# A log-sum-exp kernel: loads of one size first, more single rows last, one activation table, and results stored in two column blocks

## The chip, the core and the metric

The kernel runs on one core of a Trainium2 chip. The time is device time of one execution in microseconds (us). The profile of an execution covers a span that is about 1.8 us shorter than that time: the profiled execution of the kernel before took 169.63 us and has a span of 167.86 us. Engines that matter here: ScalarE (ACT in the profile) computes the exponentials, VectorE (DVE) sums, SyncE (SP) issues the DMAs.

## The reference

The input is 32 x 512 rows of 1024 float32 values, 67.1 MB. For each row the result is the logarithm of the sum of exponentials.

```python
max_x = np.max(x, axis=-1, keepdims=True)
return (max_x.squeeze(-1) + np.log(np.sum(np.exp(x - max_x), axis=-1))).astype(np.float32)
```

Both kernels leave the maximum out. The values are normally distributed, so the exponentials don't overflow.

## The kernel before

Each of the 128 partitions holds 128 rows. The rows are loaded in chunks into a pool of ten buffers. A chunk of one row takes one Exp with an accumulated sum. Chunks of two or four rows are processed in pairs: one Exp runs over two rows and accumulates the sum of both, VectorE sums the first row alone, and one subtract at the end gives all the second sums. Then come two Lns and four stores.

```python
    head = [1, 1, 2, 2]
    tail = [2, 2, 2, 2, 1, 1]
    # ... sizes = head + [4] * 28 + tail; xs is a pool of 10 buffers
    for c0, rpc in sched:
        x_tile = xs.tile([P, RPC, D], fp32)
        nc.sync.dma_start(out=x_tile[:, 0:rpc, :], in_=x3[:, c0 : c0 + rpc, :])
        if rpc == 1:
            nc.scalar.activation(..., func=AF.Exp,
                accum_out=sums3[:, c0 // 2, (c0 % 2) : (c0 % 2) + 1])
            continue
        for k in range(rpc // 2):
            # ... Exp over rows lo, lo+1, accum_out=pair_buf[:, j : j + 1]
            # ... nc.vector.reduce_sum of row lo into sums3[:, j, 0:1]
    # ... one tensor_sub for all pairs; Ln over 126 columns, Ln over 2 columns
    for q in range(4):
        eng = nc.scalar if (q % 2 == 0) else nc.sync
        # ... eng.dma_start of 32 partitions x 128 columns (512 bytes a row)
```

The softmax here doesn't subtract the row's maximum and nothing guards it: scores larger than these inputs give would overflow.

## Time and profile before

| | before |
|---|---|
| median time | 169.27 us (169.19 to 169.29, 3 runs) |
| profiled execution: time, span | 169.63 us, 167.86 us |
| ScalarE, VectorE busy | 76%, 45% of the span |
| end of the input stream | 160.78 us |
| end of the last Exp with its accumulator read | 162.89 us |
| issue of the last result stores begins | 164.63 us |

The first fence has lines of the page of the kernel before: DMA busy tenths and GB/s in 40 slices of the span, the chain that ended last, and two groups of instructions (busy us, mean ns; then idle us of the engine before them and what ended it).

```profile
DMA  5999999999999999999999999999999999999910
GB/s 172 387 445 426 437 429 433 437 418 426 429 429 429 429 437 422 429 420 429 429 429 437 422 426 426 429 428 429 433 426 426 426 429 426 433 412 420 404 41 16
...
DMA x_tile<-in_x_dram 83%; ACT x_tile L72 8%; SPq L57 2%; DVE sums L78 2%; ACT x_tile L60 1%; ACT L95 1%; ACT result_buf L95 0%; ACT result_buf L101 0%; ACTq L72 0%
...
L72 ACT ACTIVATE x_tile<-x_tile 128x2048 f32<-128x2048 f32 x62 | 117.8, 1901 | 33.3 <-DMA x_tile<-in_x_dram 33.3
...
L95 ACT ACT_TABLE_LOAD x1 | 1.3, 1283 | 0.0
```

The DMA is full from the second slice to the 38th, at about 428 GB/s, and the chain is 83% input DMA. ScalarE spends 33.3 us waiting for input: it is faster than the stream. So the stream sets the length, and only what comes before it is at full rate and after its last byte can be shortened. A second table load (L95) of 1283 ns stands before the first Ln.

The next fence is the tail of the kernel before, from the timeline: start, duration, engine, line, operation; in brackets the idle time before it and what ended that.

```profile
158.81 1.91 ACT L72 ACTIVATE x_tile<-x_tile 128x2048 f32<-128x2048 f32 x1 [0.39 <-DMA x_tile<-in_x_dram]
...
160.72 1.04 ACT L60 ACTIVATE x_tile<-x_tile 128x1024 f32<-128x1024 f32 x1
...
161.76 1.04 ACT L60 ACTIVATE x_tile<-x_tile 128x1024 f32<-128x1024 f32 x1
...
162.70 0.19 ACT L60 ACTIVATION_READ_ACCUMULATOR x_tile<-x_tile 128x1 f32 x1
162.91 1.28 ACT L95 ACT_TABLE_LOAD   x1
164.20 0.31 ACT L95 ACTIVATE result_buf<-sums 128x126 f32<-128x126 f32 x1
164.42 0.19 ACT L101 ACTIVATE result_buf<-sums 128x2 f32<-128x2 f32 x1
164.63 0.82 SPq L111 DMA_DIRECT2D out_dram<-result_buf  x2
164.63 0.87 ACTq L111 DMA_DIRECT2D out_dram<-result_buf  x2
```

The last wait for data ends at 158.81 us. After that ScalarE has one pair and two single rows to do, loads a table, runs two Lns, and only then are the stores issued. Two windows of the stream (length, busy time by engine, clock, DMA share, GB/s):

```profile
20.00:50.00 30.00, 14.99 (x13) 23.53 (x26) 0.00 (x0) 1.00 1.01 430
50.00:100.00 50.00, 25.25 (x21) 39.40 (x41) 0.00 (x0) 1.00 1.01 428
```

### The profile page before, as it was taken

The page shows a single profiled execution, that of the slowest core. Times are in us where ns is not written, and L with a number is a line of the kernel's source. Part 1 is how long each engine was busy: PE and PEld are TensorE (multiplying, and loading weights), DVE is VectorE, ACT ScalarE, POOL GpSimd, SP SyncE. Part 2 cuts the span into 40 slices and gives each one's busy share as a digit, 9 for nine tenths or more (in the row PEclk, how much of TensorE's full clock was granted, in tenths as well). Part 3 has the DMA queues.
Part 4 walks back from the last instruction along what each step waited for, and adds up shares of the span by engine and source line. Part 5 has one row for each costly group of instructions (what it writes and reads, how often), then busy time and mean ns, then how long its engine had stood idle before and what let it go on. Part 6 is the DMA issues. An engine that isn't in the chain of part 4 may idle for free.

```text
span 167.9 us, 372 instructions
## 1 busy us (share of the span) xinstructions
DVE 75.8 (45%) x63; ACT 128.1 (76%) x136; POOL 0.2 (0%) x4
## 2 busy tenths in 40 slices
DVE  0022445445544544554454455444455544446630
ACT  3573897777789777778977777896777798779992
POOL 0000000000000000000000000000000000000000
DMA  5999999999999999999999999999999999999910
GB/s 172 387 445 426 437 429 433 437 418 426 429 429 429 429 437 422 429 420 429 429 429 437 422 426 426 429 428 429 433 426 426 426 429 426 433 412 420 404 41 16
DMA packets 5666, 67.19 MB, mean 400 GB/s; under 512 B 672, under 2 KB 800, under 8 KB 1312
## 3 DMA queue, kind: packets, MB, share of 16 engines
q1 hardware_dynamic: 5568, 67.14, 94.9%
q10 hardware_dynamic: 96, 0.03, 0.1%
q14 instruction: 2, 0.02, 0.0%
HBM read 67.11 MB, written 0.07 MB: 400 GB/s over the span
## 4 chain that ended last, share of the span: by engine, by line
DMA 83%; ACT 10%; SPq 2%; DVE 2%; issue 1%; ACTq 0%
DMA x_tile<-in_x_dram 83%; ACT x_tile L72 8%; SPq L57 2%; DVE sums L78 2%; ACT x_tile L60 1%; ACT L95 1%; ACT result_buf L95 0%; ACT result_buf L101 0%; ACTq L72 0%
## 5 line engine op out<-in xcount | busy, mean ns | idle before, releaser
L72 ACT ACTIVATE x_tile<-x_tile 128x2048 f32<-128x2048 f32 x62 | 117.8, 1901 | 33.3 <-DMA x_tile<-in_x_dram 33.3
L78 DVE TENSOR_REDUCE sums<-x_tile 128x1 f32<-128x1024 f32 x62 | 75.6, 1220 | 86.5 <-ACT x_tile L72 86.5
L72 ACT ACTIVATION_READ_ACCUMULATOR x_tile<-x_tile 128x1 f32 x62 | 11.6, 186 | 0.0
L60 ACT ACTIVATE x_tile<-x_tile 128x1024 f32<-128x1024 f32 x4 | 4.2, 1048 | 2.5 <-DMA x_tile<-in_x_dram 2.4
L60 ACT ACT_TABLE_LOAD x1 | 1.3, 1283 | 0.7 <-PEq L129 0.7
L95 ACT ACT_TABLE_LOAD x1 | 1.3, 1283 | 0.0
L60 ACT ACTIVATION_READ_ACCUMULATOR x_tile<-x_tile 128x1 f32 x4 | 0.7, 187 | 0.0
L95 ACT ACTIVATE result_buf<-sums 128x126 f32<-128x126 f32 x1 | 0.3, 308 | 0.0
L87 DVE TENSOR_TENSOR sums<-pair_buf,sums 128x62 f32<-128x62 f32 x1 | 0.2, 227 | 0.0
L101 ACT ACTIVATE result_buf<-sums 128x2 f32<-128x2 f32 x1 | 0.2, 187 | 0.0
L129 POOL MEMSET const-bfloat16-1.0<- 128x1 bf16 x1 | 0.1, 102 | 0.0
L129 POOL MEMSET const-uint8-127<- 128x1 uint8 x1 | 0.1, 102 | 0.0
L129 POOL MEMSET const-float32-1.0<- 128x1 f32 x1 | 0.1, 99 | 0.0
L129 POOL MEMSET const-float32-0.0<- 128x1 f32 x1 | 0.1, 98 | 0.2 <-issue 0.2
## 6 DMA issues: line engine op xcount, KB each, us to landing
x_tile<-in_x_dram SPq DMA_DIRECT2D x28, 2048.0 KB, 39.1
x_tile<-in_x_dram SPq DMA_DIRECT2D x6, 1024.0 KB, 30.7
x_tile<-in_x_dram SPq DMA_DIRECT2D x4, 512.0 KB, 13.3
out_dram<-result_buf SPq DMA_DIRECT2D x2, 16.0 KB, 1.5
out_dram<-result_buf ACTq DMA_DIRECT2D x2, 16.0 KB, 1.6
```

The costliest lines, as they stand in the source:

```text
L57: nc.sync.dma_start(out=x_tile[:, 0:rpc, :], in_=x3[:, c0 : c0 + rpc, :])
L60: nc.scalar.activation(out=x_tile[:, 0, :], in_=x_tile[:, 0, :], func=AF.Exp, accum_out=sums3[:, c0 // 2, (c0 % 2) : (c0 % 2) + 1],)
L72: nc.scalar.activation(out=x_tile[:, lo : lo + 2, :], in_=x_tile[:, lo : lo + 2, :], func=AF.Exp, accum_out=pair_buf[:, j : j + 1],)
L78: nc.vector.reduce_sum(out=sums3[:, j, 0:1], in_=x_tile[:, lo, :], axis=X,)
L87: nc.vector.tensor_sub(out=sums3[:, first_p : last_p + 1, 1], in0=pair_buf[:, first_p : last_p + 1], in1=sums3[:, first_p : last_p + 1, 0],)
L95: nc.scalar.activation(out=result_buf[:, 0:split_col], in_=sums_flat[:, 0:split_col], func=AF.Ln,)
L101: nc.scalar.activation(out=result_buf[:, split_col:rows_per_part], in_=sums_flat[:, split_col:rows_per_part], func=AF.Ln,)
L129: nc = _bacc.Bacc("TRN2", target_bir_lowering=False, num_devices=1)
```

## The change

The change intends to shorten both ends. It starts with 4-row loads, ends with four single rows instead of two, loads one table set that holds Exp and Ln before anything else, finishes the first 96 columns in the middle of the stream (own buffers, subtract, Ln), and leaves 32 columns for the end. The results go out in two stores on SyncE, the first of which is issued before the end.

```diff
-    head = [1, 1, 2, 2]
-    tail = [2, 2, 2, 2, 1, 1]
+    N_BULK = 29
+    N_TAPER = 4
+    N_SINGLE = 4
+    A_CHUNKS = 24
 ...
+    nc.scalar.preload_act_table_set("natural_log_exp_and_others")
+    # 24 chunks of 4 rows, into sumsA and pairA
+    nc.vector.tensor_sub(out=sumsA[:, :, 1], in0=pairA, in1=sumsA[:, :, 0])
+    nc.scalar.activation(out=resultA, in_=sumsA, func=AF.Ln)
+    # 5 chunks of 4 rows, 4 of 2 rows into sumsC and pairC, one tensor_sub,
+    # 4 single rows into sumsC
+    nc.scalar.activation(out=resultC, in_=sumsC, func=AF.Ln)
 ...
-    for q in range(4):
-        eng = nc.scalar if (q % 2 == 0) else nc.sync
-        p0 = q * PQ
-        eng.dma_start(out=out_view[p0 : p0 + PQ, :], in_=result_buf[p0 : p0 + PQ, :])
+    nc.sync.dma_start(out=out_view[:, 0:A_COLS], in_=resultA)
+    nc.sync.dma_start(out=out_view[:, A_COLS:rows_per_part], in_=resultC)
```

More of the change, by code (lines that the diff above doesn't have):

```diff
@@ L32, with load, do_pair_chunk @@
     RPC = 4
-    head = [1, 1, 2, 2]
-    tail = [2, 2, 2, 2, 1, 1]
-    n_bulk = (rows_per_part - sum(head) - sum(tail)) // RPC
-    assert sum(head) + n_bulk * RPC + sum(tail) == rows_per_part
-    sizes = head + [RPC] * n_bulk + tail
-    sched = []
-    c = 0
-    for s in sizes:
-        sched.append((c, s))
-        c += s
-        assert s == 1 or c % 2 == 0, "pair-style chunks must stay pair aligned"
-    singles = ctx.enter_context(tc.tile_pool(name="singles", bufs=1))
-    sums3 = singles.tile([P, n_pairs, 2], fp32)
-    pair_buf = singles.tile([P, n_pairs], fp32)
-    result_buf = singles.tile([P, rows_per_part], fp32)
-    pair_style = [False] * n_pairs
+    N_BULK = 29
+    N_TAPER = 4
+    N_SINGLE = 4
+    assert N_BULK * RPC + N_TAPER * 2 + N_SINGLE == rows_per_part
+    A_CHUNKS = 24
+    A_PAIRS = A_CHUNKS * RPC // 2
+    C_PAIRS = n_pairs - A_PAIRS
+    A_COLS = 2 * A_PAIRS
+    singles = ctx.enter_context(tc.tile_pool(name="singles", bufs=1))
+    sumsA = singles.tile([P, A_PAIRS, 2], fp32)
+    pairA = singles.tile([P, A_PAIRS], fp32)
+    resultA = singles.tile([P, 2 * A_PAIRS], fp32)
+    sumsC = singles.tile([P, C_PAIRS, 2], fp32)
+    pairC = singles.tile([P, C_PAIRS], fp32)
+    resultC = singles.tile([P, 2 * C_PAIRS], fp32)
     xs = ctx.enter_context(tc.tile_pool(name="xs", bufs=10))
-    for c0, rpc in sched:
+    def load(c0, rpc):
         x_tile = xs.tile([P, RPC, D], fp32)
         nc.sync.dma_start(out=x_tile[:, 0:rpc, :], in_=x3[:, c0 : c0 + rpc, :])
-        if rpc == 1:
-            nc.scalar.activation(
-                out=x_tile[:, 0, :],
-                in_=x_tile[:, 0, :],
-                func=AF.Exp,
-                accum_out=sums3[:, c0 // 2, (c0 % 2) : (c0 % 2) + 1],
-            )
-            continue
+        return x_tile
+    def do_pair_chunk(x_tile, c0, rpc):
         for k in range(rpc // 2):
             j = c0 // 2 + k
-            pair_style[j] = True
+            if j < A_PAIRS:
+                sums, pair, jj = sumsA, pairA, j
+            else:
+                sums, pair, jj = sumsC, pairC, j - A_PAIRS
             lo = 2 * k
@@ L75 @@
                 func=AF.Exp,
-                accum_out=pair_buf[:, j : j + 1],
+                accum_out=pair[:, jj : jj + 1],
             )
             nc.vector.reduce_sum(
-                out=sums3[:, j, 0:1],
+                out=sums[:, jj, 0:1],
                 in_=x_tile[:, lo, :],
@@ L82 @@
             )
-    first_p = pair_style.index(True)
-    last_p = len(pair_style) - 1 - pair_style[::-1].index(True)
-    assert all(pair_style[first_p : last_p + 1])
+    nc.scalar.preload_act_table_set("natural_log_exp_and_others")
+    for i in range(A_CHUNKS):
+        c0 = i * RPC
+        do_pair_chunk(load(c0, RPC), c0, RPC)
     nc.vector.tensor_sub(
-        out=sums3[:, first_p : last_p + 1, 1],
-        in0=pair_buf[:, first_p : last_p + 1],
-        in1=sums3[:, first_p : last_p + 1, 0],
-    )
-    split_col = 2 * (last_p + 1)
-    sums_flat = sums3.rearrange("p j s -> p (j s)")
-    nc.scalar.activation(
-        out=result_buf[:, 0:split_col],
-        in_=sums_flat[:, 0:split_col],
-        func=AF.Ln,
-    )
-    if split_col < rows_per_part:
+        out=sumsA[:, :, 1],
+        in0=pairA,
+        in1=sumsA[:, :, 0],
+    )
+    nc.scalar.activation(out=resultA, in_=sumsA, func=AF.Ln)
+    for i in range(A_CHUNKS, N_BULK):
+        c0 = i * RPC
+        do_pair_chunk(load(c0, RPC), c0, RPC)
+    for t in range(N_TAPER):
+        c0 = N_BULK * RPC + 2 * t
+        do_pair_chunk(load(c0, 2), c0, 2)
+    C_BULK_PAIRS = C_PAIRS - N_SINGLE // 2
+    nc.vector.tensor_sub(
+        out=sumsC[:, 0:C_BULK_PAIRS, 1],
+        in0=pairC[:, 0:C_BULK_PAIRS],
+        in1=sumsC[:, 0:C_BULK_PAIRS, 0],
+    )
+    for r in range(N_SINGLE):
+        c0 = N_BULK * RPC + 2 * N_TAPER + r
+        jj = c0 // 2 - A_PAIRS
+        x_tile = load(c0, 1)
         nc.scalar.activation(
-            out=result_buf[:, split_col:rows_per_part],
-            in_=sums_flat[:, split_col:rows_per_part],
-            func=AF.Ln,
-        )
-    PQ = P // 4
-    for q in range(4):
-        eng = nc.scalar if (q % 2 == 0) else nc.sync
-        p0 = q * PQ
-        eng.dma_start(
-            out=out_view[p0 : p0 + PQ, :],
-            in_=result_buf[p0 : p0 + PQ, :],
-        )
+            out=x_tile[:, 0, :],
+            in_=x_tile[:, 0, :],
+            func=AF.Exp,
+            accum_out=sumsC[:, jj, (c0 % 2) : (c0 % 2) + 1],
+        )
+    nc.scalar.activation(out=resultC, in_=sumsC, func=AF.Ln)
+    nc.sync.dma_start(out=out_view[:, 0:A_COLS], in_=resultA)
+    nc.sync.dma_start(out=out_view[:, A_COLS:rows_per_part], in_=resultC)
 _INS = ['x']
```

## The prediction

> **What bounds the kernel now.** The 67.1 MB input load. In the page's 40 slices the DMA row is full from the second slice to the thirty-eighth; the windows view shows 428 to 433 GB/s from 20 to 140 us. The waits view agrees: ScalarE waits 33.3 us for input, about 1 us per 2 MB tile, and the chain of waits is 83% input DMA. A row per partition arrives every 1.22 us (0.52 MB at 428 GB/s); ScalarE takes 0.95 us for it in a pair, 1.04 us alone. So only the head before full bandwidth and the tail after the last bytes can be shortened.
>
> Head (windows, 2 to 12 us): 391 GB/s on average, with loads of 1, 1, 2 and 2 rows first.
> Tail (timeline): the DMA thins out from 159.2 and stops near 160.8 us; the last pair of Exps starts at 158.81 (the last wait for DMA), two single Exps follow without a wait and end at 162.89; a table load takes 1.28 us, two Lns run 164.20 to 164.61, the stores are issued from 164.63 (two per queue, about 0.41 us each), and the span ends at 167.9.
>
> **What the change does.**
> - One table set with both Exp and Ln is loaded first; the table load before Ln goes: -1.28 us, all on the critical path. The Trainium skill (ScalarE: Activation LUTs, Table sets) says `natural_log_exp_and_others` holds both; its page gives a switch as about 1283 ns of load plus 1380 ns of drain. This trace has the 1.28 us but no such drain: the load starts 0.02 us after the last accumulator read.
> - Two final Lns become one over 32 columns: -0.2 us.
> - Four single rows last in place of two: the last pair lands about 2.5 us sooner. Estimate: pair at 156.3, then singles of 1.04 us, ending near 162.4: -0.45 us.
> - Head of 2 MB loads only: ScalarE starts near 7 us instead of 4.4, which is free, as it has slack. At 428 instead of 391 GB/s the first 10 us would give -0.4 us (uncertain; part of it is ramp).
> - Output: two stores on the SP queue. The first (96 columns) is issued behind the loads and is off the path. The second has one issue in place of two: -0.4 us. But its rows are 128 bytes, before 512: DMA: Bandwidth & Descriptors (Specifications) says that below 512 bytes the engine does read-modify-write; no run shows its cost yet; I allow +0.2 us.
> - The mid-stream subtract and Ln: ScalarE waits about 1.6 us (reduce 1.22, subtract 0.23, signals) and works 0.3 us. Loads keep eight DMAs in flight with ten buffers, so this doesn't stop the stream: 0.
>
> Sum: -1.28 - 0.2 - 0.45 - 0.4 - 0.4 + 0.2 = -2.5 us.
>
> **Predicted** 166.8 us, 80% range 165.8 to 168.0. Faster by over 2% (under about 165.95 us) 0.13; within 2% 0.86; slower 0.01.
>
> **What would show each step.** One table load in the groups, at the start. From the end of the last Exp to the issue of the last store 0.3 us instead of 1.74. From that issue to the end about 2.9 us instead of 3.3. DMA rate unchanged at 428 in the middle; the DMA stops near 160.4. ScalarE waits about 1.6 us once, near 125 us, and catches up within two tiles with no dip of GB/s. The last Exp ends near 162.
>
> **What would make it wrong.** Starting with 2 MB loads raises the rate more, or not at all; the small stores complete much later than I allow; the single rows arrive late at the tail (the engines finish unevenly), so each Exp waits; the mid-stream stall reaches the stream.

## The result

The changed kernel took 167.51 us (median; 166.89 to 167.78, 12 runs), the kernel before 169.27 us (169.01 to 170.61, 15 runs). The ratio is 0.9875, with a 95% interval of 0.9854 to 0.9896: within 2%, and inside the predicted range of 165.8 to 168.0 us. Ratios here are the mean time of one kernel's fast runs over that of the other's of the same rounds, so they are not quite the ratio of the medians. All outputs are right.

Lines of the page after, as those of before, with one more group:

```profile
DMA  5999999999999999999999999999999999999980
GB/s 198 423 435 427 419 391 431 427 431 380 399 435 423 431 431 435 427 427 421 435 435 419 431 427 435 427 425 423 435 427 423 427 431 431 423 411 423 406 325 4
...
DMA x_tile<-in_x_dram 89%; ACT x_tile L66 3%; SPq L55 2%; ACT x_tile L110 2%; DVE sumsA L72 1%; ACT resultC L117 0%; ACTq L66 0%
...
L78 ACT ACT_TABLE_LOAD x1 | 1.3, 1283 | 0.7 <-PEq L135 0.7
L89 ACT ACTIVATE resultA<-sumsA 128x96 f32<-128x96 f32 x1 | 0.3, 283 | 1.5 <-DVE sumsA L84 1.5
```

The only table load is now at the start (L78). The Ln of the first 96 columns (L89) waited 1.5 us for VectorE. But the GB/s line has three weak slices: 391, then 380 and 399, where the kernel before has none below 418 in the middle. The windows after:

```profile
20.00:50.00 30.00, 14.53 (x12) 22.52 (x23) 0.00 (x0) 1.00 1.00 411
50.00:100.00 50.00, 24.66 (x21) 39.95 (x43) 0.00 (x0) 1.00 1.01 429
```

From 20 to 50 us the stream ran at 411 GB/s instead of 430. At 411 GB/s that stretch of 30 us moved 0.57 MB less, an estimated 1.3 us of the stream. The timeline of the tail after:

```profile
156.91 1.91 ACT L66 ACTIVATE x_tile<-x_tile 128x2048 f32<-128x2048 f32 x1 [0.38 <-DMA x_tile<-in_x_dram]
...
158.82 1.04 ACT L110 ACTIVATE x_tile<-x_tile 128x1024 f32<-128x1024 f32 x1
...
161.99 1.06 ACT L110 ACTIVATE x_tile<-x_tile 128x1024 f32<-128x1024 f32 x1
162.95 0.19 ACT L110 ACTIVATION_READ_ACCUMULATOR x_tile<-x_tile 128x1 f32 x1
163.17 0.23 ACT L117 ACTIVATE resultC<-sumsC 128x32 f32<-128x32 f32 x1
163.42 0.34 SPq L120 DMA_DIRECT2D out_dram<-resultC  x1
```

There is no table load any more. From the end of the last accumulator read (162.95 + 0.19 = 163.14) to the issue of the last store pass 0.28 us; before it was 1.74. From that issue to the end of the span pass 2.31 us; before it was 3.23. Yet the last Exp ends later than before (163.14 against 162.89): the stream ended at 161.44 us, and I had expected 160.4.

So three things were left to explain: what made the stream late, why the end after the last store became 0.92 us shorter and not 0.4, and whether the head gave anything.

### The profile page after: what moved, and what is told of

It reads as the page before. It is cut to its first block, busy times and chain, and to the rows that moved or that the text cites. A ratio compares the mean times of both kernels' runs of the same rounds, so it can differ in the third digit from the quotient of the medians.

```text
span 165.7 us, 368 instructions
## 1 busy us (share of the span) xinstructions
DVE 76.0 (46%) x64; ACT 126.5 (76%) x135; POOL 0.2 (0%) x4
## 4 chain that ended last, share of the span: by engine, by line
DMA 89%; ACT 5%; SPq 2%; issue 2%; DVE 1%; ACTq 0%
DMA x_tile<-in_x_dram 89%; ACT x_tile L66 3%; SPq L55 2%; ACT x_tile L110 2%; DVE sumsA L72 1%; ACT resultC L117 0%; ACTq L66 0%
## 5 line engine op out<-in xcount | busy, mean ns | idle before, releaser
L72 DVE TENSOR_REDUCE sumsA<-x_tile 128x1 f32<-128x1024 f32 x48 | 58.5, 1220 | 69.1 <-ACT x_tile L66 69.1
L72 DVE TENSOR_REDUCE sumsC<-x_tile 128x1 f32<-128x1024 f32 x14 | 17.1, 1220 | 15.2 <-ACT x_tile L66 15.2
L78 ACT ACT_TABLE_LOAD x1 | 1.3, 1283 | 0.7 <-PEq L135 0.7
L89 ACT ACTIVATE resultA<-sumsA 128x96 f32<-128x96 f32 x1 | 0.3, 283 | 1.5 <-DVE sumsA L84 1.5
```

Source lines behind the costliest of these rows:

```text
L72: nc.vector.reduce_sum(out=sums[:, jj, 0:1], in_=x_tile[:, lo, :], axis=X,)
L78: nc.scalar.preload_act_table_set("natural_log_exp_and_others")
L89: nc.scalar.activation(out=resultA, in_=sumsA, func=AF.Ln)
```

## The experiments

Twelve kernels ran (two of them the changed kernel again), in three calls of four; each call ran on one chip, a different one each time, and repeated the kernel before. The table was worked out from the traces of the profiled executions: the end of the last input packet ("stream end"), and then the three pieces of the tail: to the end of the last accumulator read, to the start of the last issue group of result stores, to the end of the span. "Slow packets" counts 16 KB packets of over 750 ns after the first 12 us (the usual one takes 0.61 us); two of them stand in every profile, each 0.3 us after an 8 KB packet of the instruction queue. "SyncE records" counts SyncE's instructions in the trace. Further down, a store has landed when the last of its completion signals has arrived.

| run | median us | profiled us | stream end | to last Exp | to store issue | to end | slow packets | SyncE records |
|---|---|---|---|---|---|---|---|---|
| before | 169.27 | 169.63 | 160.78 | 2.11 | 1.74 | 3.23 | 2 | 81 |
| changed | 167.51 | 167.51 | 161.44 | 1.70 | 0.29 | 2.31 | 30 | 78 |
| r_after (call 1; before there 169.13) | 166.38 | 166.38 | 160.30 | 1.70 | 0.29 | 2.30 | 2 | 78 |
| e_table | 167.62 | 168.55 | 161.09 | 2.14 | 0.32 | 3.22 | 2 | 81 |
| e_head | 166.87 | 166.84 | 160.30 | 1.69 | 0.29 | 2.80 | 2 | 84 |
| e_4stores | 167.12 | 167.15 | 160.52 | 1.68 | 0.29 | 2.89 | 2 | 78 |
| r2_after (call 2; before there 169.26) | 166.45 | 166.52 | 160.45 | 1.70 | 0.29 | 2.31 | 2 | 78 |
| e_split | 166.42 | 166.47 | 160.48 | 1.69 | 0.29 | 2.27 | 2 | 80 |
| e_headb | 167.35 | 167.35 | 160.79 | 1.70 | 0.28 | 2.80 | 2 | 84 |
| e_1store | 166.78 | 166.54 | 160.29 | 1.68 | 0.29 | 2.50 | 2 | 77 |
| e_split6 (call 3; before there 169.78) | 168.17 | 168.51 | 161.77 | 1.69 | 0.29 | 2.98 | 9 | 84 |
| e_headact | 166.95 | 167.04 | 160.97 | 1.71 | 0.29 | 2.29 | 10 | 79 |
| e_tail2 | 167.68 | 167.50 | 160.86 | 2.09 | 0.29 | 2.36 | 22 | 76 |
| e_tail6 | 167.19 | 167.23 | 161.21 | 1.69 | 0.29 | 2.29 | 34 | 80 |

### The late stream: the changed kernel again (r_after, r2_after)

Theory A: the stalls of the stream are chance, and come with the chip or the moment. Theory B: the start with 4-row loads brings them.

> The changed kernel again, for a second profile. Its first profile lost 1.3 us against the kernel before between 20 and 50 us: at 23.7 and at 40.5 us eight 16 KB packets at a time took 1.4 to 2.25 us instead of 0.61. Theory A (chance): the stalls fall elsewhere or are missing this time, and the executions scatter over 0.9 us as they did (166.9 to 167.8). Theory B (the 2 MB start puts the engines into a bad phase): stalls of the same size at about the same places, 20 to 50 us, again. Ratio to the kernel before about 0.988 either way.

> The changed kernel a third time, to compare the others of this call with on the same chip, and a third look for stalls of the load stream (first profile: two, worth 1.3 us; second: none). If they are chance: mostly none, 166.3 to 166.5 us. If they return with the same chip or the same program: 167.5 us again.

The unchanged file took 166.38 us (ratio to before 0.9822, 0.9794 to 0.985, where I had expected 0.988 either way) and 166.45 us (0.983, 0.9814 to 0.9846): 1.1 us less than the first time. Neither profile has a stall like those; the windows of r_after:

```profile
20.00:50.00 30.00, 15.10 (x13) 24.00 (x27) 0.00 (x0) 1.00 1.01 429
```

429 GB/s stand where the first profile had 411. Theory B as I had put it falls: the same program shows nothing of the kind in two later calls, on two chips. The third call, on a third chip, had stalls in all four of its profiles (9 to 34 slow packets), although these were four different kernels, and the kernel before was slower there too (median 169.78, up to 170.52 us, against 169.13 and 169.26). So the stalls come and go with the call. A weaker form of theory B is not excluded: that the change makes stalls more frequent where they occur. In the first measurement all twelve executions of the changed kernel were slow (166.89 us at least, against 166.59 at most in r_after), while the kernel before had its usual median there (169.27, though with single executions up to 170.61). And of the profiles with stalls, those that start with 4-row loads (changed, e_tail2, e_tail6) have 22 to 34 slow packets, those whose first loads are smaller (e_split6, e_headact) 9 and 10, with one profile of each. What causes the stalls no trace shows. The expectation that a quiet execution takes 166.3 to 166.5 us held.

The tail of r_after ends like this:

```profile
161.82 0.19 ACT L110 ACTIVATION_READ_ACCUMULATOR x_tile<-x_tile 128x1 f32 x1
162.03 0.23 ACT L117 ACTIVATE resultC<-sumsC 128x32 f32<-128x32 f32 x1
162.29 0.34 SPq L120 DMA_DIRECT2D out_dram<-resultC  x1
```

### The table set alone (e_table)

```diff
+    nc.scalar.preload_act_table_set("natural_log_exp_and_others")
     xs = ctx.enter_context(tc.tile_pool(name="xs", bufs=10))
```

> The kernel before with only the common table set loaded first. If the table load before Ln lies wholly on the critical path: 1.28 us less, ratio 0.9924, about 168.0 us, Ln straight after the last accumulator read, no drain in its place. If the load hid another wait (the subtract, the last accumulator), less than 1 us.

It took 167.62 us, 1.51 us under the 169.13 of the same call (ratio 0.9907, 0.988 to 0.9934). The timeline of its tail:

```profile
163.04 0.19 ACT L62 ACTIVATION_READ_ACCUMULATOR x_tile<-x_tile 128x1 f32 x1
163.14 0.29 ACT L97 ACTIVATE result_buf<-sums 128x126 f32<-128x126 f32 x1
163.34 0.19 ACT L103 ACTIVATE result_buf<-sums 128x2 f32<-128x2 f32 x1
163.55 0.83 SPq L113 DMA_DIRECT2D out_dram<-result_buf  x2
```

Without the table load, the first Ln starts at 163.14, before the last accumulator read ends at 163.04 + 0.19 = 163.23; in the kernel before, the load started only after that read (162.89, then 162.91). So the piece from the last Exp to the issue shrank from 1.74 to 0.32 us, by 1.42: the 1.28 of the load and 0.09 of this overlap make up nearly all of it. The whole load was on the critical path. The rest of the 1.51 lies within the scatter of the executions (167.57 to 168.55; the profiled one was the slowest). In the changed kernel the piece is 0.29: there the one Ln needs the last row and can't overlap, but it takes 0.23 us where the two Lns of before took 0.41 (164.20 to 164.61).

### The head (e_head, e_headb)

```diff
-    for i in range(A_CHUNKS):
-        c0 = i * RPC
+    # e_head: two single rows, then loads of 2, 2, 2 rows
+    # (e_headb: two single rows, then 2, 2, and 4-row chunks from row 6 on)
+    for i in range(2, A_CHUNKS):
+        c0 = i * RPC
         do_pair_chunk(load(c0, RPC), c0, RPC)
```

> The changed kernel with the first 8 rows loaded as 1, 1, 2, 2, 2 instead of two times 4. If the 2 MB head gives the 0.4 us of the prediction (0.57 us ahead at 20 us in the first profile): 0.4 to 0.6 us slower than the changed kernel. Theory B of the stalls: no stalls between 20 and 50 us, which gives back 1 us or more, so it is 0.5 to 0.8 us faster than the changed kernel and its executions scatter less. Theory A: stalls as often as in the changed kernel.

> The changed kernel with exactly the head of before (1, 1, 2, 2, so that the 4-row loads start at row 6). e_head (1, 1, 2, 2, 2) ended its load stream at 160.3 us like the changed kernel, while before and e_table were 0.13 to 0.23 MB behind at 20 us, with dips to 300 GB/s between 5 and 8 us. If the head of before costs it: dips again, stream ends 0.3 to 0.5 us later than in e_head, total 0.8 to 1.0 us over the changed kernel (0.45 of it the SyncE pause). If those dips were chance: as e_head, 0.45 to 0.5 over.

e_head was 0.49 us slower than r_after, about what the head term of my prediction said, but for another reason. Its stream ended at 160.30 us, as that of r_after did; its last store was issued at 162.27 us against 162.29. All the difference lies after that issue: 2.80 us against 2.30. Without the stages this run would have passed for a proof of the head term.

e_headb took 167.35 us, 0.90 over r2_after. Of this, 0.49 is again after the last issue, and 0.34 is a later end of the stream (160.79 against 160.45). The dips between 5 and 8 us that before and e_table have did not come back (421 GB/s there, against 371 and 370). The windows of the first 20 us clear the small loads themselves: e_headb and e_head moved 381 GB/s in them, r_after 381 and r2_after 377, before 369. e_headb fell behind only later (427 GB/s against 430 of r2_after from 20 to 50 us, 424 against 426 from 100 to 150 us), and all four of its executions were slow (167.28 to 167.40 us). Whether the fifth 2-row load near its end or the 4-row chunks that start at row 6 do this stays open.

### What happens after the last issue (e_split, e_split6, e_headact)

In the trace of SyncE the waits after the last store look like this; first r_after, then e_head (start us, ns, operation, awaited semaphores), with the landing of the last store in both:

```
r_after                                   e_head
163.71 last landing                       163.69 last landing
163.723   28  wait 107, 100               162.819  897  wait 107, 100
163.787   28  wait 108, 99                163.758   28  wait 108, 99
163.855    7  drain                       164.204  130  drain           <- record 79
163.919    7  drain, signal               164.395    7  drain, signal
```

The stores land at the same time, but in e_head SyncE stands still for 0.42 us before the drain, which then takes 130 ns instead of 7. The semaphore that this drain waits for (102) does not change in this time. In the same way before and e_table have a pause of 0.45 and 0.46 us late in their end sequence. Counted from zero, it is always record 79 of SyncE that comes late: in before, e_table, e_head and e_headb. The changed kernel has 78 records, and never reaches it. That was theory S; theory H held that the small first loads themselves cost the half microsecond. The end-sequence instructions of SyncE, by their source line (ns shortest/median/longest, first and last start), in r_after and in e_head:

```profile
L146 SPq EVENT_SEMAPHORE  x6: 17/28/28, 162.7 to 164.5; - x6
...
L146 SPq DRAIN  x3: 7/7/7, 163.9 to 164.2; - x3
```

```profile
L156 SPq EVENT_SEMAPHORE  x6: 17/28/897, 162.7 to 165.0; - x6
...
L156 SPq DRAIN  x3: 7/7/130, 164.2 to 164.6; - x3
```

The longest drain, 130 ns, is the one behind the pause. (The 897 ns wait is an ordinary wait for the last landing.) Three runs tested this. e_split and e_split6 leave the bytes and the tiles alone, and only issue early loads as two DMAs:

```diff
-        nc.sync.dma_start(out=x_tile[:, 0:rpc, :], in_=x3[:, c0 : c0 + rpc, :])
+        step = 2 if c0 < 2 * RPC else rpc        # e_split6: 6 * RPC
+        for r in range(0, rpc, step):
+            nc.sync.dma_start(out=x_tile[:, r : r + step, :],
+                              in_=x3[:, c0 + r : c0 + r + step, :])
```

> The changed kernel, its first two loads issued as two DMAs of 2 rows each: 4 records more on SyncE (82 instead of 78), the same bytes. Theory S: SyncE pauses about 0.45 us just before its 80th record (number 79 from zero: seen there in before, e_table and e_head, each with over 80 records), and the changed kernel escapes it because it has only 78: then the DMA stream ends at the same time and the kernel is 0.4 to 0.5 us slower, with the gap on SyncE after the last store. Rival H (e_head was slower because of its small first loads): this kernel has no loads of one row and is at most 0.15 us slower, without a gap.

> As the run with two split loads, but with the first six loads split into two DMAs of 2 rows. That run had 80 records on SyncE (not the 82 I had counted), so its last record was the one that pauses in other kernels, and it told nothing. This one should have 84, as e_head. Theory S (SyncE pauses about 0.4 us before its record number 79): issue of the late store to the end of the span is 2.7 to 2.8 us instead of 2.3 to 2.25, with a gap of about 0.42 us before record 79, and the kernel is 0.4 to 0.5 us slower than the changed kernel (166.4). Rival H (one-row loads at the head cost e_head its 0.5 us): no gap, within 0.15 us of the changed kernel.

e_split couldn't decide by its time: I had miscounted, it has 80 records, so record 79 is its last, and it took 166.42 us, as r2_after did. The gap before that record was 0.44 us. A final handshake of the engines takes 0.36 us there in the kernels that don't reach record 79, so the pause can lie mostly hidden beneath it and cost 0.08 us. e_tail6 (below) also has 80 records and the same 0.44 us, which fits theory S.

e_split6 has 84 records, and there record 79 is again a late drain: 0.43 us after the record before it, 117 ns long.

```profile
L151 SPq DRAIN  x3: 7/7/117, 165.9 to 166.3; - x3
```

From its last issue to the end pass 2.98 us, more than the 2.7 to 2.8 expected: about 0.17 of that is that three waits follow the landing there, where r_after has one. Its total of 168.17 us can't be compared with 166.4, as its stream had stalls (end 161.77); the gap decides here, not the total.

e_headact is e_head with its first five loads issued by ScalarE, which leaves 79 records on SyncE:

```diff
+        queue = nc.scalar if c0 < 8 else nc.sync
+        queue.dma_start(
+    head = [load(0, 1), load(1, 1), load(2, 2), load(4, 2), load(6, 2)]
     nc.scalar.preload_act_table_set("natural_log_exp_and_others")
```

> e_head (first loads of 1, 1, 2, 2, 2 rows) with those five loads issued from ScalarE's queue, so that SyncE has 79 records. Theory S: no gap on SyncE at the end, and 0.4 to 0.5 us faster than e_head's 166.87, so about 166.4, as the changed kernel. Rival H: as slow as e_head, 166.8 to 166.9.

```profile
L158 SPq DRAIN  x3: 7/7/7, 164.5 to 164.8; - x3
```

No drain is long now, no gap, and 2.29 us to the end, as in the changed kernel, with the same small first loads. Its median of 166.95 us misses the expected 166.4; the stream ended at 160.97 us, 0.67 later than in e_head, and on this chip the streams had stalls. Theory H falls by both runs, by the pieces of the span rather than by the totals. What makes SyncE pause at that record is open. A fetch of instructions is a candidate: the Trainium skill (Runtime: NRT & Kernel Launch, Instruction fetch mechanics) describes refills in blocks of 256 instructions. The traces of before and e_head show no packet of the instruction queue within the pause, and record 79 is no block boundary that I could derive from that page. But an 8 KB packet of that queue starts 0.62 to 0.65 us after record 79 has begun in all five kernels with the pause (0.88 and 0.92 us in e_tail6 and e_split, where the record is the last). That ties the two together in time; it doesn't show which causes which.

### The stores (e_4stores, e_1store)

```diff
 # e_4stores: one result tile, and the four stores of before
+    for q in range(4):
+        eng = nc.scalar if (q % 2 == 0) else nc.sync
+        eng.dma_start(out=out_view[p0 : p0 + PQ, :], in_=result_buf[p0 : p0 + PQ, :])
 # e_1store: one result tile, and one store
+    nc.sync.dma_start(out=out_view, in_=result_buf)
```

> The changed kernel with the four stores of before (32 partitions of 512 bytes each, two queues). The profiles gave 2.3 us from the issue of the last store to the end after, and 3.2 before. If the stores are the cause: 0.9 us slower than the changed kernel (ratio about 0.993 to before). If 128-byte rows cost what they save (my prediction allowed 0.2 us): the difference is only 0.2 to 0.4 us.

> The changed kernel with one result tile and one store of 128 x 512 bytes after the last Ln, instead of an early store of 96 columns and a late one of 32 columns (128-byte rows). If rows under 512 bytes cost my allowance of 0.2 us: 0.1 to 0.3 us faster, issue to landing under 1.4 us. If the 16 KB of the late store against 64 KB matters: 0.1 to 0.2 us slower. My guess is within 0.1 us.

e_4stores took 167.12 us, 0.74 over r_after. It has 78 records and no pause. From issue to end pass 2.89 us against 2.30:

```profile
162.49 0.83 SPq L122 DMA_DIRECT2D out_dram<-result_buf  x2
162.49 0.87 ACTq L122 DMA_DIRECT2D out_dram<-result_buf  x2
```

Of the 0.59, 0.41 is the issue of the second store on the same queue (162.49 and 162.90 us); most of the rest is that ScalarE's second store lands last, 1.64 us after its issue, where r_after's store takes 1.42. The stream end of that one profile, 0.22 us later, makes up the rest of the 0.74. So the four stores cost 0.59 us, which lies between my two expectations (0.9, and 0.2 to 0.4). Before has the same four stores and takes 3.23; the 0.34 that are left are not theirs.

e_1store took 166.78 us (166.54 to 166.97), 0.33 over r2_after with more scatter; from issue to end pass 2.50 us against 2.31. Its 64 KB in rows of 512 bytes take 1.55 us from issue to landing, the 16 KB in rows of 128 bytes of r2_after 1.43 us. These two differ in bytes as well as in rows. With equal bytes, the first store on SyncE in e_4stores (16 KB in rows of 512 bytes) takes 1.42 us, as long as the store in rows of 128 bytes (1.42 us in r_after). So the 0.2 us that I had allowed for short rows is not there.

### The tail (e_tail2, e_tail6)

```diff
-    N_TAPER = 4
-    N_SINGLE = 4
+    N_TAPER = 5        # e_tail6: 3
+    N_SINGLE = 2       # e_tail6: 6
```

> The changed kernel with five 2-row loads and two single rows at the end, instead of four and four. My prediction gave four singles 0.45 us over two. Then: last Exp ends 0.4 to 0.5 us later after the last data of the stream (2.1 us as in before, 1.7 in the changed kernel), 166.8 to 166.9 in all.

> The changed kernel with three 2-row loads and six single rows at the end. ScalarE waits 0.4 us before the last pair of the changed kernel, and two singles take it 0.18 us longer than a pair: at best 0.2 us faster (166.2), at worst 0.1 us slower; I expect within 0.15 us of the changed kernel, as the last single there already waits for its data.

With two single rows the last Exp ends 2.09 us after the stream, with four 1.69 to 1.71, with six 1.69. The timeline of e_tail2 shows why:

```profile
158.87 1.91 ACT L66 ACTIVATE x_tile<-x_tile 128x2048 f32<-128x2048 f32 x1 [0.49 <-DMA x_tile<-in_x_dram]
...
160.78 1.04 ACT L110 ACTIVATE x_tile<-x_tile 128x1024 f32<-128x1024 f32 x1
...
161.81 1.04 ACT L110 ACTIVATE x_tile<-x_tile 128x1024 f32<-128x1024 f32 x1
...
162.76 0.19 ACT L110 ACTIVATION_READ_ACCUMULATOR x_tile<-x_tile 128x1 f32 x1
```

A pair that waited for its data until 158.87 is followed by two rows that had landed meanwhile; with four singles a smaller part is left at that point. So four singles give 0.4 us, and six nothing more. The totals of this call (167.68 and 167.19 us) carry the stalls of that chip, and the totals alone would not have shown this.

### Not tried

No run took the early subtract and Ln out of the changed kernel. The timeline and the windows of r_after answer for it:

```profile
125.02 0.18 ACT L66 ACTIVATION_READ_ACCUMULATOR x_tile<-x_tile 128x1 f32 x1
126.73 0.28 ACT L89 ACTIVATE resultA<-sumsA 128x96 f32<-128x96 f32 x1 [1.53 <-DVE sumsA L84]
...
131.11 1.91 ACT L66 ACTIVATE x_tile<-x_tile 128x2048 f32<-128x2048 f32 x1 [0.31 <-DMA x_tile<-in_x_dram]
```

```profile
120.00:125.00 5.00, 2.44 (x2) 3.99 (x5) 0.00 (x0) 1.00 1.01 429
125.00:130.00 5.00, 2.49 (x3) 3.47 (x6) 0.00 (x0) 1.00 1.00 426
130.00:135.00 5.00, 2.60 (x3) 4.69 (x6) 0.00 (x0) 1.00 1.02 433
```

ScalarE waits 1.53 us for VectorE, starts the next tile without a wait, waits 0.31 us instead of the usual 1 us before the one after that (131.11), and so has caught up; the stream stays at 426 to 433 GB/s. No version that was tried beats the changed kernel: e_split is equal (166.42 against 166.45 us), the others are slower or can't be told apart on their chip.

## Why the prediction was right

The total was right, both in the first measurement (167.51) and without stalls (166.38 and 166.45), against 166.8 predicted. The terms, with what they measured where the stream was quiet:

| term | predicted us | measured us | from |
|---|---|---|---|
| table load and second Ln | -1.28 - 0.2 | -1.45 | to store issue, 1.74 to 0.29; e_table alone -1.42 |
| four single rows | -0.45 | -0.4 | to last Exp, 2.11 to 1.70; e_tail2 2.09 |
| result stores | -0.4 + 0.2 | -0.59 | to end, e_4stores 2.89 to r_after 2.30 |
| pause of SyncE | not foreseen | -0.34 | to end, before 3.23 to e_4stores 2.89 |
| head | -0.4 | about 0, at most -0.5 | stream end, see below |
| early subtract and Ln | 0 | 0 | windows of r_after |
| stalls of the stream | not foreseen | +1.1, first measurement only | 167.51 against 166.38 and 166.45 |

- **The table term was right** in its sum: 1.48 predicted, 1.45 measured. Its parts hold too: 1.28 for the load, and 0.18 for one Ln of 0.23 us in place of two of 0.41. The Trainium skill (ScalarE: Activation LUTs, What ACT_TABLE_LOAD costs) gives 1283 ns for the load, which is exactly what the groups show; the drain that it adds was in none of these traces (of which only that of before has a switch of sets, before its first Ln).
- **The tail term was right**: 0.45 predicted, 0.4 measured.
- **The store term was mis-sized**: I wrote that from the last issue to the end about 2.9 us would pass; it was 2.3, a gain of 0.93. The stores are 0.59 of it, by e_4stores: the missing issue gave its 0.41, and the landing of ScalarE's second store most of the rest. The allowance for rows of 128 bytes, made because DMA: Bandwidth & Descriptors (Specifications) tells of read-modify-write below 512 bytes, was wrong here: these rows landed 1.42 us after the issue, and so did 512-byte ones of the same total size. The other 0.34 is the difference between before and e_4stores, and 0.28 of it can be read in the trace of before as the pause of SyncE before record 79, which the shorter SyncE program escapes: the gap there is 0.38 us longer than in r_after and the drain 0.12, but the final handshake behind it is 0.21 shorter. (In e_head nothing of the pause is hidden, and it costs 0.50.) No reading of the diff could have told that, and it is no merit of the change's idea.
- **The head term was not confirmed.** The profile of before ends its stream at 160.78 us and r_after at 160.30, a gain of 0.48; but that execution of before took 169.63 us, 0.5 more than the median of 169.13 in call 1. If I take that 0.5 off, the three tail pieces (0.41 + 1.45 + 0.93 = 2.79) explain the whole difference of the medians, 169.13 - 166.38 = 2.75, and nothing is left for the head. e_head agrees with that (stream end 160.30, as without small loads), and so do the first 20 us of e_headb, which has the head of before and lost its time later. So the head is most likely worth nothing; as before was profiled only once, a part of the 0.48 is not excluded.
- **The stalls were missing from the prediction.** They hid 1.1 us of the gain in the first measurement. That 167.51 us lies in the range is partly the luck of two unforeseen terms with opposite signs: the stalls, and the pause that was saved. The sum without stalls has luck of its own: the 0.4 that the head didn't give is what the stores gave beyond their term (0.59 instead of 0.2).
- Other marks of the prediction: the stream should stop near 160.4 us (160.30 and 160.45 without stalls, 161.44 in the first profile), the last Exp end near 162 (162.00 and 162.15; first 163.14), ScalarE wait 1.6 us near 125 us (1.53, at 126.7). All hold where the stream is undisturbed.

## What to carry to other kernels

When a stream of loads sets the length, cut the trace at the end of the stream, at the last compute and at the last store's issue, and compare these pieces; totals of an experiment can agree with a theory for a reason that lies in another piece, as e_head did. Load a table set that holds every function of the kernel at the start, issue one small store at the end, and feed the last rows in small pieces only until the engine waits for its data again. Run a first result again on another chip before looking in the code for a loss in the middle of a stream.

## What the Trainium skill lacked or had wrong

- ScalarE: Activation LUTs (What ACT_TABLE_LOAD costs) adds about 1380 ns of drain to a switch of the table. Here the second load took 1283 ns and started 0.02 us after the accumulator read, and leaving it out gave 1.42 us in the trace (1.51 in the medians): the load and a small overlap, but no such drain.
- DMA: Bandwidth & Descriptors (Specifications) names 512 bytes as the least size for full rate. For the one store that is waited for at the end this cost nothing visible: 128 rows of 128 bytes landed after 1.42 to 1.43 us, 32 rows of 512 bytes (the same bytes in all) after 1.42 us, 128 rows of 512 bytes after 1.55 us.
- Runtime: NRT & Kernel Launch (Instruction fetch mechanics) gives no pause of the kind seen on SyncE: 0.41 to 0.46 us, always before its record 79, in every profile with more than 80 records (before, e_table, e_head, e_headb, e_split6), which cost 0.50 us in e_head, where it falls behind the last wait, and about 0.3 us in before.
- I found no page that explains the stalls of the load stream: in the first profile of the changed kernel eight 16 KB packets at a time took 1.4 to 2.25 us instead of 0.61. They came in some calls and not in others, and the calls with them were 0.5 to 1.1 us slower for the same kernel (before in call 3: 169.78 against 169.26 and 169.13; changed in the first measurement: 167.51 against 166.38, though before had 169.27 there).
